# Final norm of a two-layer block: result tile split by token halves, six stores of other sizes, and eight products of ones behind the sums

## The chip, the cores and the metric

The kernel runs on one core of one Trainium2 chip. The metric is the device time of one execution in microseconds. The kernel before takes 2117.86 us (median of 3 runs, 2117.08 to 2118.18). One further execution was profiled; its own time was 2118.3 us, of which 2116.5 us lie between its first and its last instruction (the span).

## The reference

The model has 256 tokens and a width of 2048, all in float32. Layer 0 is a mixer of a 31-tap causal convolution and a multi-scale pooling, then a SwiGLU with 5632 hidden columns. Layer 1 is a gated 3-tap convolution mixer and another SwiGLU. A last RMS norm follows:

```python
def rms_norm(x, g):
    xf = x.astype(jnp.float32)
    y = xf * lax.rsqrt(jnp.mean(xf * xf, axis=-1, keepdims=True) + EPS)
    return (y * g.astype(jnp.float32)).astype(x.dtype)

def reference(...):
    h = x
    for i in range(DEPTH):
        h = h + (conv_pool_mixer(h, ...) if i % 2 == 0 else short_conv_mixer(h, ...))
        h = h + swiglu(rms_norm(h, ffn_norm[i]), w_gate[i], w_up[i], w_down[i])
    return rms_norm(h, final_norm)
```

## The kernel before

**Data.** Activations lie transposed: partition p holds feature 128·c + p of chunk c, and the 256 tokens run along the free axis. `h` is one tile of 128 x 16 chunks x 256 tokens. The output has the same form, so one partition's row in memory is 16 chunks of 256 tokens, 16 KB.

**Weights and main products.** All weights come as 128x128 blocks in the order of use, loaded by SP (`fetch`, L102). Pieces of 8 blocks are split into a rounded part `hi` (ScalarE, L112) and the rest `lo` (VectorE, or GpSimd for part of the first mixer, L119). TensorE multiplies with hi and lo, in three products of 256 columns (L164 to L166) or in two of 512 and 256 columns (L161 and L162). Steps off the main path are put into queues in the code and released as products are issued; the final order on each engine is made by a scheduler that simulates the program, so a small change of one operation can move others.

**Norms.** A norm does not scale its tokens before the products. It collects squares per chunk (`Norm.square`), sums them over the partitions by small products with a tile of ones (`rsqrt_of`, L235: one column per half of the tokens, so token t sits on partition t of column 0 or 1), and computes 1/sqrt there on 2 columns (`spread_over`, L242 to L249): ScalarE takes a square root, VectorE the reciprocal `y`, and one Newton step e = y·(1.5 − 0.5·var·y²). To bring the values back to the free axis, VectorE multiplies the identity by `e` into the tile `diag` (L253, one half of the tokens each) and TensorE multiplies ones with `diag`: one product of 256 columns for the inner norms (`over_features`, L261), two of 128 columns for the last one (L255, `half`), so that each half of the tokens has its own PSUM tile. `spread_over` serves all norms, the layer norm of the first mixer too (`ln_rstd`). A float32 product of this kind is two MATMUL records in the trace.

**The end of the program.** The down projection of the last SwiGLU adds its result to `h` chunk by chunk. The gain of the last norm is multiplied into `h` on the way (L275), so only the factor per token is missing. After the last chunk: add (L311), square (L289), four sum records, the chain of small steps, the two `half` products, and then (L590) VectorE multiplies `h` in place, in ten pieces. Pieces of chunks 0 and 1 come first, one for each half of the tokens, each stored by its own DMA (L594); then chunks 2-3, 4-7, 8-11 and 12-15, two pieces of VectorE for one DMA (L599). `tc.issue_after` holds the order of the pieces. SP issues all six stores.

The program begins with nine products of ones (L214, `WARM`), whose result nobody reads, while the first data is on its way.

Of the kernel before, what the change touches and what calls it, by code (L numbers as in the profile page):

```python
# [3 lines left out]

# [66 lines left out]
AHEAD = 1  # L71

WARM = 9

POOL_SPLIT = range(96, 24 * NC + 16 + 7 * NC + 8)

# [6 lines left out]
def block_kernel(ctx: ExitStack, tc: tile.TileContext, xT: bass.AP, xtok: bass.AP, vec: bass.AP, wall: bass.AP, out: bass.AP):  # L83
    nc = tc.nc
# [4 lines left out]
    tmp = ctx.enter_context(tc.tile_pool(name="tmp", bufs=2))  # L89
    ps = ctx.enter_context(tc.tile_pool(name="ps", bufs=5, space=PSUM))  # L90
# [116 lines left out]
    h = act.tile([P, NC, T], F32, name="h")  # L207
    xs = act.tile([P, NC, 2 * T], F32R, name="xs")
    ones = const.tile([P, P], F32, name="ones")
    nc.gpsimd.memset(ones, 1.0)  # L210

    idle = ps_st.tile([P, P], F32, name="idle", tag="st")
    for _ in range(WARM):
        nc.tensor.matmul(idle, ones, ones, start=True, stop=True)  # L214
# [11 lines left out]
    def rsqrt_of(*totals, scale, halves=False, st=None):  # L226

        small = ps_st.tile([P, 8], F32, name="st", tag="st")  # L230
        if st is None:
            st = small[:, :2]
        for i, x in enumerate(totals):
            for j in range(2):
                nc.tensor.matmul(st[:, j : j + 1], x[:, j * P : (j + 1) * P], ones[:, :1], start=i == j == 0, stop=i == len(totals) - 1, skip_group_check=True)  # L235
        return spread_over(small, st, scale, halves)

    def spread_over(small, st, scale, halves=False):

        var, root, e = (small[:, 2 * i : 2 * i + 2] for i in range(1, 4))  # L240
        y = tmp.tile([P, 2], F32, name="inv", bufs=1)
        nc.scalar.activation(root, st, AF.Sqrt, scale=scale, bias=eps)  # L242
        nc.vector.tensor_scalar(out=var, in0=st, scalar1=scale, scalar2=EPS, op0=ALU.mult, op1=ALU.add)
        nc.vector.reciprocal(y, root)
        for j in range(2):
            yj = y[:, j : j + 1]
            nc.vector.scalar_tensor_tensor(out=e[:, j : j + 1], in0=var[:, j : j + 1], scalar=yj, in1=yj, op0=ALU.mult, op1=ALU.mult)
        nc.vector.tensor_scalar(out=e, in0=e, scalar1=-0.5, scalar2=1.5, op0=ALU.mult, op1=ALU.add)
        nc.vector.tensor_tensor(out=e, in0=e, in1=y, op=ALU.mult)  # L249
        diag = tmp.tile([P, T], F32, name="diag", tag="sq")  # L250
        spread = [ps.tile([P, P], F32, name="half", tag="acc") for _ in range(2)] if halves else None
        for j in range(2):
            nc.vector.tensor_tensor(out=diag[:, j * P : (j + 1) * P], in0=identity, in1=e[:, j : j + 1].broadcast_to([P, P]), op=ALU.mult)  # L253
            if halves:
                nc.tensor.matmul(spread[j], ones, diag[:, j * P : (j + 1) * P], start=True, stop=True)  # L255
        return spread or over_features(diag)

    def over_features(x):

        st = ps_st.tile([P, T], F32, name="st", tag="st")  # L260
        nc.tensor.matmul(st, ones, x, start=True, stop=True)  # L261
        return st

    class Norm:
# [95 lines left out]
    with tc.tile_pool(name="m0", bufs=1) as m0, tc.tile_pool(name="ps_side", bufs=2, space=PSUM) as ps_side:  # L360
# [223 lines left out]
    last = Norm("final_norm", final=True)  # L584
    swiglu(norm, last)
    halves = rsqrt_of(*last.sums, scale=1.0 / D, halves=True)

    def normed(at, n, j):
        part = h[:, at : at + n, j * P : (j + 1) * P]
        return nc.vector.tensor_tensor(out=part, in0=part, in1=halves[j].unsqueeze(1).broadcast_to([P, n, P]), op=ALU.mult).ins  # L590

    for j in range(2):
        start = normed(0, 2, j)
        nc.sync.dma_start(out[:, :2, j * P : (j + 1) * P], h[:, :2, j * P : (j + 1) * P])  # L594
    for at, n in ((2, 2), (4, 4), (8, 4), (12, 4)):
        with tc.issue_after(start):
            for j in range(2):
                start = normed(at, n, j)
        nc.sync.dma_start(out[:, at : at + n, :], h[:, at : at + n, :])  # L599


def _blocks(w):
# [78 lines left out]
```

## Time and profile before

| | before |
|---|---|
| median of 3 runs | 2117.86 us (2117.08 to 2118.18) |
| the profiled execution's own time | 2118.3 us |
| its span | 2116.5 us |
| TensorE (PE) busy | 2091.5 us, 99% |
| VectorE (DVE) busy | 1382.9 us, 65% |
| ScalarE (ACT) busy | 1060.6 us, 50% |
| GpSimd (POOL) busy | 200.7 us, 9% |
| last product of the last projection ends | 2103.0 us after the span's start |
| TensorE clock granted, mean | 0.995 |

Times in the trace count from the span's start. PE is TensorE's products, PEld its weight loads, SPq the issues of DMAs by SP. A row of the timeline gives start, duration, engine, line, operation, tiles and shapes, how many instructions were merged into the row, and in brackets how long the engine had been idle and for whom it waited. A row of a table by stretches gives, for each stretch, its length and each engine's busy time with the number of instructions, then the granted TensorE clock (1.00 is full), the busy share of the DMA engines and GB/s.

### The profile page before, as it was taken

Reading aid. Unit: us, or ns where it says so; the run is one execution under the profiler, and the core shown is the slowest. Engines: PE = TensorE matmul, PEld = TensorE weight load, DVE = VectorE, ACT = ScalarE, POOL = GpSimd, SP = SyncE. Lnnn points to the kernel's source line nnn. Section 1 sums busy time; section 2 is a strip of 40 time slices with the busy share of each in tenths; the row PEclk is TensorE's granted clock in tenths of the full one; section 3 lists DMA queues with packets and bytes.
Section 4 is the critical chain, followed back from the end, with each engine's and each line's share of the span. In section 5 each row is a group of like instructions: output and inputs, shape, how many; then the busy total and the mean of one; then the engine's idle time right before and its main releaser. Section 6 shows DMA issues by size and latency. Waiting matters only on the chain.

```text
span 2116.5 us, 31578 instructions
## 1 busy us (share of the span) xinstructions
PE 2091.5 (99%) x12568; PEld 1860.0 (88%) x12568; DVE 1382.9 (65%) x1983; ACT 1060.6 (50%) x1571; POOL 200.7 (9%) x180
## 2 busy tenths in 40 slices
PE   8999999999999999999999999999999999999997
PEld 8999988888888888888888888888888888888887
DVE  6888766666556666666777777766665556666554
ACT  7776654444444444454444445554444444444453
POOL 3985200000000000011000001100000000000011
PEclk9999999999999999999999999999999999999999
DMA  8554455555555555455455555555555555555551
GB/s 324 190 189 170 149 181 198 181 197 182 196 180 194 184 182 196 180 186 192 179 194 185 197 183 196 180 186 193 190 189 191 187 188 191 179 191 187 181 193 64
DMA packets 57140, 395.53 MB, mean 187 GB/s; under 512 B 6432, under 2 KB 7456, under 8 KB 10016
## 3 DMA queue, kind: packets, MB, share of 16 engines
q1 hardware_dynamic: 56992, 393.52, 52.0%
q8 instruction: 98, 1.61, 0.3%
q14 instruction: 50, 0.41, 0.1%
HBM read 391.39 MB, written 2.10 MB: 186 GB/s over the span
## 4 chain that ended last, share of the span: by engine, by line
PE 98%; DVE 1%; DMA 1%; ACT 0%; SPq 0%; issue 0%; DVEq 0%; ACTq 0%
PE acc L161 57%; PE acc L162 29%; PE acc L164 4%; PE acc L166 4%; PE acc L165 4%; DMA rows<-in_xtok 0%; DMA h<-in_xT 0%; DVE h L590 0%; ACT hi L112 0%; PE st L235 0%; PE st L261 0%; DVE lo L119 0%; SPq L102 0%; ACT conv L468 0%; DVE conv L423 0%
## 5 line engine op out<-in xcount | busy, mean ns | idle before, releaser
L112 ACT CAST hi<-w 128x1024 fp32r<-128x1024 f32 (+1 forms) x740 | 775.1, 1048 | 990.7 <-PE acc L161 628.0
L119 DVE TENSOR_TENSOR lo<-w,hi 128x1024 fp32r<-128x1024 f32 (+1 forms) x691 | 845.2, 1224 | 651.2 <-ACT hi L112 647.1
L161 PE MATMUL acc<-xs,hi 128*128 128x512 f32 x3584 | 1253.9, 395 | 0.0
L162 PE MATMUL acc<-xs,lo 128*128 128x256 f32 x3584 | 1005.4, 281 | 0.0
L161 PEld LDWEIGHTS acc<-xs,hi 128*128 128x128 f32 x3584 | 671.8, 187 | 155.3
L162 PEld LDWEIGHTS acc<-xs,lo 128*128 128x128 f32 x3584 | 677.8, 189 | 0.1
L161 PE MATMUL acc<-y,hi 128*128 128x512 f32 x1386 | 486.7, 395 | 0.0
L162 PE MATMUL acc<-y,lo 128*128 128x256 f32 x1386 | 389.3, 281 | 0.0
L161 PEld LDWEIGHTS acc<-y,hi 128*128 128x128 f32 x1386 | 260.4, 188 | 61.0
L162 PEld LDWEIGHTS acc<-y,lo 128*128 128x128 f32 x1386 | 260.1, 188 | 0.4
L291 POOL TENSOR_TENSOR sumsq<-sumsq,sq 128x256 f32<-128x256 f32 x56 | 59.0, 1054 | 1612.6 <-ACT sq L289 1612.6
L164 PE MATMUL acc<-xs,hi 128*128 128x256 f32 x512 | 144.0, 284 | 5.5 <-ACT hi L112 4.3
L165 PE MATMUL acc<-xs,hi 128*128 128x256 f32 x512 | 143.6, 283 | 0.0
L166 PE MATMUL acc<-xs,lo 128*128 128x256 f32 x512 | 141.2, 284 | 0.1
L119 POOL TENSOR_TENSOR lo<-w,hi 128x1024 fp32r<-128x1024 f32 x49 | 119.1, 2452 | 43.4 <-PE acc L165 34.5
L164 PEld LDWEIGHTS acc<-xs,hi 128*128 128x128 f32 x512 | 98.0, 192 | 6.6 <-ACT hi L112 5.2
L165 PEld LDWEIGHTS acc<-xs,hi 128*128 128x128 f32 x512 | 98.1, 192 | 0.0
L166 PEld LDWEIGHTS acc<-xs,lo 128*128 128x128 f32 x512 | 96.5, 192 | 0.5 <-DVE lo L119 0.5
L161 PE MATMUL acc<-z,hi 128*128 128x512 f32 x256 | 89.4, 394 | 0.0
L186 ACT COPY cross<-acc 128x256 f32<-128x256 f32 x224 | 81.0, 362 | 0.0
L162 PE MATMUL acc<-z,lo 128*128 128x256 f32 x256 | 71.7, 281 | 0.0
L311 DVE TENSOR_TENSOR h<-acc,h 128x256 f32<-128x256 f32 x112 | 47.3, 423 | 19.9 <-PE acc L166 14.1
(131 smaller groups left out, 1201.1 us busy)
## 6 DMA issues: line engine op xcount, KB each, us to landing
w<-in_wall SPq DMA_DIRECT2D x365, 1024.0 KB, 4.8
w<-in_wall SPq DMA_DIRECT2D x7, 512.0 KB, 7.9
rows<-in_xtok SPq DMA_DIRECT2D x2, 1024.0 KB, 7.8
h<-in_xT SPq DMA_DIRECT2D x7, 256.0 KB, 7.3
out<-h SPq DMA_DIRECT2D x3, 512.0 KB, 2.8
v<-in_vec SPq DMA_DIRECT2D x1, 260.0 KB, 6.6
h<-in_xT SPq DMA_DIRECT2D x2, 128.0 KB, 2.4
w<-in_wall SPq DMA_DIRECT2D x1, 256.0 KB, 4.0
```

What stands on the lines that cost most here:

```text
L112: nc.scalar.copy(hi[:, : n * P], w)
L119: engine.tensor_tensor(out=lo[:, : n * P], in0=w, in1=hi[:, : n * P], op=ALU.subtract)
L161: nc.tensor.matmul(acc, hi, x, start=first, stop=False, skip_group_check=True)
L162: nc.tensor.matmul(acc[:, T:], lo, x[:, :T], start=False, stop=last, skip_group_check=True)
L164: nc.tensor.matmul(acc[:, :T], hi, x[:, :T], start=first, stop=False)
L165: nc.tensor.matmul(acc[:, :T], hi, x[:, T:], start=False, stop=False)
L166: nc.tensor.matmul(acc[:, :T], lo, x[:, :T], start=False, stop=last)
L186: nc.scalar.copy(t, acc[:, T:])
L291: nc.gpsimd.tensor_tensor(out=self.sums[0], in0=self.sums[0], in1=sq, op=ALU.add)
L311: nc.vector.tensor_tensor(out=h[:, n, :], in0=acc[:, :T], in1=h[:, n, :], op=ALU.add)
```

## The change

Four things are edited.

1. `rsqrt_of`, only where `halves` is set (the last norm): behind the sum products, TensorE gets `KEEP` = 8 products of ones with ones, 128 columns each, into a PSUM tile of their own that nobody reads. `tc.issue_after` puts them behind the last sum product.
2. `spread_over`, for every norm: the two VectorE instructions of one column each (var·y·y with y as a per-partition scalar) become two instructions of two columns each (y·y into a new tile, then var times that).
3. The end: the result goes to a new tile `res` of 128 x 2 halves x 16 chunks x 128 tokens, not in place. VectorE works through the first half of the tokens in pieces of 2, 6 and 8 chunks, then the second in 8, 6 and 2. Each piece has its own store, with 1, 3, 4, 4, 3 and 1 KB per partition.
4. The output in memory is 128 x 2 x 16 x 128; the host puts the axes back.

```diff
+KEEP = 8
...
         for i, x in enumerate(totals):
             for j in range(2):
-                nc.tensor.matmul(st[:, j : j + 1], x[:, j * P : (j + 1) * P], ones[:, :1], start=i == j == 0, stop=i == len(totals) - 1, skip_group_check=True)
+                mm = nc.tensor.matmul(st[:, j : j + 1], x[:, j * P : (j + 1) * P], ones[:, :1], start=i == j == 0, stop=i == len(totals) - 1, skip_group_check=True)
+        if halves:
+
+            idle = ps.tile([P, P], F32, name="idle", tag="acc")
+            with tc.issue_after(mm.ins):
+                for _ in range(KEEP):
+                    nc.tensor.matmul(idle, ones, ones, start=True, stop=True)
         return spread_over(small, st, scale, halves)
...
-        y = tmp.tile([P, 2], F32, name="inv", bufs=1)
+        y, yy = (tmp.tile([P, 2], F32, name=n, bufs=1) for n in ("inv", "inv2"))
...
-        for j in range(2):
-            yj = y[:, j : j + 1]
-            nc.vector.scalar_tensor_tensor(out=e[:, j : j + 1], in0=var[:, j : j + 1], scalar=yj, in1=yj, op0=ALU.mult, op1=ALU.mult)
+        nc.vector.tensor_tensor(out=yy, in0=y, in1=y, op=ALU.mult)
+        nc.vector.tensor_tensor(out=e, in0=var, in1=yy, op=ALU.mult)
...
-    def normed(at, n, j):
-        part = h[:, at : at + n, j * P : (j + 1) * P]
-        return nc.vector.tensor_tensor(out=part, in0=part, in1=halves[j].unsqueeze(1).broadcast_to([P, n, P]), op=ALU.mult).ins
-
-    for j in range(2):
-        start = normed(0, 2, j)
-        nc.sync.dma_start(out[:, :2, j * P : (j + 1) * P], h[:, :2, j * P : (j + 1) * P])
-    for at, n in ((2, 2), (4, 4), (8, 4), (12, 4)):
-        with tc.issue_after(start):
-            for j in range(2):
-                start = normed(at, n, j)
-        nc.sync.dma_start(out[:, at : at + n, :], h[:, at : at + n, :])
+    with tc.tile_pool(name="fin", bufs=1) as fin:
+
+        res = fin.tile([P, 2, NC, P], F32, name="res")
+        start = None
+        for j, pieces in enumerate((((0, 2), (2, 6), (8, 8)), ((0, 8), (8, 6), (14, 2)))):
+            for at, n in pieces:
+                with tc.issue_after(start) if start is not None else nullcontext():
+                    part = h[:, at : at + n, j * P : (j + 1) * P]
+                    by = halves[j].unsqueeze(1).broadcast_to([P, n, P])
+                    start = nc.vector.tensor_tensor(out=res[:, j, at : at + n, :], in0=part, in1=by, op=ALU.mult).ins
+                nc.sync.dma_start(out[:, j, at : at + n, :], res[:, j, at : at + n, :])
```

Because the scheduler simulates the program, edit 2 also moves a few instructions elsewhere. Line numbers in the changed kernel are 2 to 14 higher than before.

On TensorE, at the first norm of the program (before; `st` is the product that spreads 1/sqrt, `acc` the main products):

```order
L164 MATMUL acc<-xs,hi 128x256
L165 MATMUL acc<-xs,hi 128x256
L166 MATMUL acc<-xs,lo 128x256
L261 MATMUL st<-diag,ones 128x256
L164 MATMUL acc<-xs,hi 128x256
```

On the same engine at the same place, the change has:

```order
L166 MATMUL acc<-xs,hi 128x256
L167 MATMUL acc<-xs,hi 128x256
L268 MATMUL st<-diag,ones 128x256
L168 MATMUL acc<-xs,lo 128x256
L166 MATMUL acc<-xs,hi 128x256
```

The spreading product stands one main product earlier. The same exchange is found at the norms before the two SwiGLUs and the second mixer; at the layer norm the order stays.

On GpSimd, in the first mixer (`sw` and `pm` are steps of the pooling, `lo` pieces of weights; before):

```order
L505 TENSOR_TENSOR sw<-sw 128x2x256
L119 TENSOR_TENSOR lo<-w,hi 128x1024 x2
L507 TENSOR_TENSOR sw<-sw,corr 128x2x15
L119 TENSOR_TENSOR lo<-w,hi 128x1024 x2
L508 TENSOR_TENSOR pm<-sw,pm 128x512
L119 TENSOR_TENSOR lo<-w,hi 128x1024 x3
L505 TENSOR_TENSOR sw<-xp 128x2x262
```

The same place on GpSimd in the change:

```order
L512 TENSOR_TENSOR sw<-sw 128x2x256
L121 TENSOR_TENSOR lo<-w,hi 128x1024 x3
L514 TENSOR_TENSOR sw<-sw,corr 128x2x15
L121 TENSOR_TENSOR lo<-w,hi 128x1024 x2
L515 TENSOR_TENSOR pm<-sw,pm 128x512
L121 TENSOR_TENSOR lo<-w,hi 128x1024 x2
L512 TENSOR_TENSOR sw<-xp 128x2x262
```

One pooling step waits behind one more weight piece; ScalarE and VectorE exchange the neighbours of that pooling group in the same stretch.

On TensorE, the end of the program (before):

```order
L166 MATMUL acc<-y,lo 128x256
L235 MATMUL st<-ones,sumsq 128x1 x2
L235 MATMUL st<-ones,sq 128x1 x2
L255 MATMUL half<-diag,ones 128x128 x2
L676 UNCONDITIONAL_BRANCH
```

The end of TensorE's program in the change:

```order
L168 MATMUL acc<-y,lo 128x256
L237 MATMUL st<-ones,sumsq 128x1 x2
L237 MATMUL st<-ones,sq 128x1 x2
L243 MATMUL idle<-ones 128x128 x8
L262 MATMUL half<-diag,ones 128x128 x2
L681 UNCONDITIONAL_BRANCH
```

The eight products of ones stand ahead of the two `half` products on an engine that works in this order.

More of the change, by code (lines that the diff above doesn't have):

```diff
@@ L1 @@
 from collections import deque
-from contextlib import ExitStack
+from contextlib import ExitStack, nullcontext
 from functools import partial
@@ L674 @@
     args = [nc.dram_tensor(f"in_{n}", a.shape, F32, kind="ExternalInput").ap() for n, a in arrays.items()]
-    args.append(nc.dram_tensor("out_0", (P, NC, T), F32, kind="ExternalOutput").ap())
+    args.append(nc.dram_tensor("out_0", (P, 2, NC, P), F32, kind="ExternalOutput").ap())
     with tile.TileContext(nc, schedule_with_timeline_sim=True) as tc:
@@ L679 @@
     got = np.asarray(r.results[0]["out_0"])
-    return np.ascontiguousarray(got.transpose(2, 1, 0)).reshape(1, T, D)
+    return np.ascontiguousarray(got.transpose(1, 3, 2, 0)).reshape(1, T, D)
```

## The prediction

> **What bounds the kernel now.** I read the page first, then the end of the timeline, then the same stretch by windows with the clock and the DMA share, and last the places where TensorE waits.
>
> From the page:
>
> ```profile
> span 2116.5 us, 31578 instructions
> PE 2091.5 (99%) x12568; PEld 1860.0 (88%) x12568; DVE 1382.9 (65%) x1983; ACT 1060.6 (50%) x1571; POOL 200.7 (9%) x180
> PE 98%; DVE 1%; DMA 1%; ACT 0%; SPq 0%; issue 0%; DVEq 0%; ACTq 0%
> ```
>
> For 99% of the span TensorE's products are the bound, and the change takes none of them away. What can move is the end behind the last main product (2103.0 to 2116.5, 13.5 us) and the few places where a norm makes TensorE wait. All that is 0.6% of the time, so the forecast is a matter of tenths of a microsecond. The timeline of the end:
>
> ```profile
> 2103.94 0.61 PE L235 MATMUL st<-ones,sq 128*128 128x1 f32 x4 [0.63 <-ACT sq L289]
> 2104.58 0.24 ACT L242 ACTIVATE st<-st,eps 128x2 f32<-128x2 f32 x1 [0.16 <-PE st L235]
> 2105.26 0.49 DVE L247 SCALAR_TENSOR_TENSOR st<-st,inv 128x1 f32<-128x1 f32 x2
> 2105.78 0.17 DVE L248 TENSOR_SCALAR st<-st 128x2 f32<-128x2 f32 x1
> 2105.98 0.17 DVE L249 TENSOR_TENSOR st<-st,inv 128x2 f32<-128x2 f32 x1
> 2106.26 0.48 DVE L253 TENSOR_TENSOR diag<-v,st 128x128 f32<-128x128 f32 x2
> 2106.66 0.93 PEld L255 LDWEIGHTS half<-diag,ones 128*128 128x128 f32 x4 [2.20 <-issue]
> 2106.69 1.20 PE L255 MATMUL half<-diag,ones 128*128 128x128 f32 x4 [2.15 <-DVE diag L253]
> 2107.50 5.10 DVE L590 TENSOR_TENSOR h<-h,half 128x256 f32<-128x256 f32 x10 [0.76 <-PE half L255]
> 2107.95 0.92 SPq L594 DMA_DIRECT2D out<-h  x2
> ```
>
> It is one chain: sums, square root, five small steps, diag, half, and then VectorE without a pause for 5.10 us. TensorE stands still for 2.15 us in it. The windows show what that does to its clock (the column behind the busy times; then DMA share and GB/s):
>
> ```profile
> core 0: us, PE busy (x) PEld busy (x) DVE busy (x) ACT busy (x) POOL busy (x), PEclk, DMA share, GB/s
> 2103.22:2106.63 3.41, 0.70 (x5) 0.53 (x5) 1.72 (x9) 1.16 (x3) 0.00 (x0) 1.00 0.00 0
> 2106.63:2110.04 3.41, 1.20 (x4) 0.93 (x4) 2.65 (x7) 0.00 (x0) 0.00 (x0) 0.50 0.29 91
> 2109.00:2110.00 1.00, 0.00 (x0) 0.00 (x0) 1.00 (x3) 0.00 (x0) 0.00 (x0) 0.50 0.87 267
> 2110.70:2111.10 0.40, 0.00 (x0) 0.00 (x0) 0.40 (x2) 0.00 (x0) 0.00 (x0) 0.50 0.15 61
> 2111.10:2112.00 0.90, 0.00 (x0) 0.00 (x0) 0.90 (x3) 0.00 (x0) 0.00 (x0) 0.50 0.97 400
> 2114.00:2115.00 1.00, 0.00 (x0) 0.00 (x0) 0.00 (x0) 0.00 (x0) 0.00 (x0) 0.50 0.91 373
> ```
>
> The clock went from 1.00 to 0.50 at 2106.63, 0.03 us ahead of the weight load of `half`: both `half` products ran at half speed. And the DMA engines, short of work up to 2111.10, are then full to the end. So the last part of the program is bound by 1.57 MB (the last three stores of 512 KB) at about 400 GB/s, counted from the moment when the first of these three is issued. Its issue, the last issue, and SP's wait for the last landing:
>
> ```profile
> 2110.23 0.34 SPq L599 DMA_DIRECT2D out<-h  x1
> 2112.66 0.33 SPq L599 DMA_DIRECT2D out<-h  x1
> SPq L676 <- DMA out<-h: 2.4, 1, 2.4
> out<-h SPq DMA_DIRECT2D x3, 512.0 KB, 2.8
> out<-h SPq DMA_DIRECT2D x2, 128.0 KB, 1.9
> ```
>
> From issue to first bytes lie 0.9 us (2110.23 to 2111.1).
>
> **The small steps (edit 2).** Before, two one-column instructions take from 2105.26 to 2105.78, 0.52 us. Now two two-column ones, each as L248, whose start lies 0.20 us ahead of the next: 0.40. **−0.12 us**. Bounds 0 (if a new tile costs a wait) and −0.15.
>
> The other norms gain this only where TensorE waits for it. At the first norm:
>
> ```profile
> 39.37 0.30 PEld L261 LDWEIGHTS st<-diag,ones 128*128 128x128 f32 x2
> 39.48 0.59 PE L261 MATMUL st<-diag,ones 128*128 128x256 f32 x2
> 41.14 0.36 PE L164 MATMUL acc<-xs,hi 128*128 128x256 f32 x1 [1.07 <-DVE gate L318]
> ```
>
> The spreading product ran right behind the main ones, so `diag` was ready; behind it TensorE stood for 1.07 us until VectorE had freed a PSUM tile. Now it stands one main product earlier, all that hangs on it comes 0.12 us earlier, which is how far apart main products are in the chain of waits there, and the displaced product fills the pause: **−0.12 us**, between 0 and −0.2:
>
> ```profile
> 39.41 0.12 PE acc L165
> ```
>
> At the layer norm (its chain of waits) a weight piece stands between, which hides the gain, **0**:
>
> ```profile
> 206.36 1.05 ACT hi L112
> 207.44 1.23 DVE lo L119
> 208.66 0.41 DVE diag L253 x2
> ```
>
> `lo` waits for `hi`, not for the small steps, and `diag` stands behind `lo`. The other three norms make TensorE wait nowhere: 0.
>
> **The products of ones (edit 1).** Their price is seen at the program's start, at a clock that was low until nearly the last of them:
>
> ```profile
> 0.99 3.70 PE L214 MATMUL idle<-ones 128*128 128x128 f32 x18 [0.99 <-POOL eps L216]
> ```
>
> Eight are 16 records. At low clock 3.70/18 makes 0.206 us each, 3.3 us in all; at full clock L261 (0.59 us for two, the second lasting 0.38) shows 0.21 us between starts at 256 columns, so 0.107 at 128, and 16 take 1.7 us. They start behind the sums at about 2104.5 and are issued by 2106.2; `half` wants to load its weights at 2106.66 − 0.12 = 2106.54. So they lie wholly beside the small steps of ScalarE and VectorE and cost nothing, with 0.3 us to spare; past that each delay goes straight into `half`.
>
> How busy TensorE must be is bounded by the other place where the clock fell, at the layer norm:
>
> ```profile
> 205.40:208.82 3.42, 0.98 (x9) 0.78 (x7) 2.96 (x10) 2.33 (x2) 0.00 (x0) 1.00 0.70 273
> 208.82:219.06 10.24, 6.46 (x26) 5.77 (x27) 5.31 (x10) 6.11 (x12) 0.00 (x0) 0.50 0.29 107
> 215.64:219.06 3.42, 3.42 (x18) 3.42 (x17) 1.90 (x3) 1.62 (x4) 0.00 (x0) 0.50 0.00 0
> ```
>
> A stretch of 3.42 us with TensorE busy for 0.98 of it, 29%, was followed by a low clock. In that of 2103.22 to 2106.63 TensorE was busy for 0.70 us, 20%; now it would be 0.70 + 1.7 = 2.4 of 3.41 us, 70%. I take it that the clock stays. Then `half`: before, from the weight load (2106.66) to VectorE's start (2107.50) 0.84 us, all but 0.04 of it TensorE. At full clock, halving gives 0.40; L261's 0.71 us (39.37 to 40.07) less 2 x 0.107 for the halved columns gives 0.50. I take 0.45: **−0.35 us** (−0.30 to −0.40; 0 if the clock falls anyway).
>
> The Trainium skill (TensorE: Matmul & The Clock Gate, "What's actually happening") has the gate watch a free-running window of 3413 ns that does not reset at the kernel's start. The trace agrees in the length, since the low stretch in the middle is 10.24 us, three such windows. By the page the step would fall elsewhere in other executions; what that does is the first rival.
>
> **The pieces (edit 3).** VectorE's rows for pieces of 512 columns, and one instruction of 1024 with another output tile than its input:
>
> ```profile
> 2109.52 3.07 DVE L590 TENSOR_TENSOR h<-h,half 128x512 f32<-128x512 f32 x5
> L119 DVE TENSOR_TENSOR lo<-w,hi 128x1024 fp32r<-128x1024 f32 (+1 forms) x691 | 845.2, 1224 | 651.2 <-ACT hi L112 647.1
> ```
>
> Five starts of 512 columns are (3.07 − 0.68)/4 = 0.60 us apart; 256 columns, from the seven starts ahead, 0.33. That is 0.07 + 1.04 ns per column: 0.87 for 768, 1.13 for 1024 columns. The sum over all is 4.7 us and not 5.1, but VectorE's end no longer decides. What counts is when the store is issued from which the DMA engines stay full. Before, 2110.20 − 2107.50 = 2.70 us behind VectorE's start. Now the third store, behind pieces of 256, 768 and 1024: 0.33 + 0.87 + 1.22 = 2.41. **−0.29 us** (with the first two stores, 0.5 MB, out just by then: the second is issued 1.3 us behind the start, and takes 0.9 + 1.0 us, until 3.2; the third's first bytes come at 3.3).
>
> From there the same 1.57 MB are left (512 + 512 + 384 + 128 KB). Each later store is issued before the one ahead is through, so the engines stay full; SP issues six stores as before, at 0.33 to 0.46 us each, and the two closest come 0.33 us apart, ahead of a full queue. Only the last 128 KB go in rows of 1 KB: the rows of 512 bytes went at 267 GB/s (2109 to 2110), rows of 4 KB at 400; between the two, 0.40 us for 0.33: **+0.05 us** (0 to +0.15).
>
> Sum: −0.12 − 0.12 − 0.35 − 0.29 + 0.05 = **−0.83 us**. Against its own execution that is a span of 2115.7 us and a time of 2117.5; against the median of the runs, which lies 0.44 us below the profiled one, 2117.86 − 0.83 = **2117.0 us**.
>
> **Rivals.**
>
> *The clock was not what the profile shows.* The step came 0.03 us ahead of `half`; a shift of the window by 0.8 us to a later time leaves `half` fast without any help, and then edit 1 brings nothing: −0.83 + 0.35 = −0.48, 2117.4 us. The same time comes out if a window that is 70% busy still loses the clock. For it: no row here shows a window between 29% and full that kept it. Against it: the profiled execution is one like the others.
>
> *The last store decides, not the throughput.* Then the end is the last issue plus its landing: VectorE's start at 2107.50 − 0.12 − 0.35 = 2107.03, 4.75 us of pieces, issue at 2111.8, and 1.9 us for 128 KB give 2113.7, against 2112.66 + 2.8 = 2115.5 before: −1.8, with the first norm −1.9, 2116.0 us. Against it: the DMA share of 0.91 to 0.97 in the last windows, which says that a store of 128 KB would queue.
> The Trainium skill (DMA: Bandwidth & Descriptors, "Rules for kernel authors") speaks against stores this small: at least 1 MiB per DMA, small ones joined. Here 512 KB in one store went at 400 GB/s, so the rows agree only for the smallest pieces. By that page's fit for one DMA (2.0 us plus the bytes at 436 GB/s, given for GpSimd's path) 128 KB would take an estimated 2.3 us and the kernel 2116.4 us in this case.
>
> *Slower: the products of ones hold `half` back.* Place: TensorE, which works in order, from 2104.5 on. If the clock falls before they are through, or they start late, `half` waits. At low clock 16 x 0.206 = 3.3 us end at 2107.8, `half` starts 1.15 us later than before and is slow: +1.15 − 0.29 + 0.05 − 0.12 = +0.8, 2118.7 us. The kernel is slower than before from the point where `half` starts 0.36 us late, that is from 0.16 us per record on. Against it: the clock was 1.00 until 2106.63, and the eight products themselves fill the window.
>
> *Slower: the moved order in the first mixer makes TensorE wait.* GpSimd now does three pieces of `lo` in a row ahead of a pooling step:
>
> ```profile
> 70.03 4.82 POOL L119 TENSOR_TENSOR lo<-w,hi 128x1024 fp32r<-128x1024 f32 x2
> PE acc L164 <- DVE xs L198: 0.9, 1, 0.9
> ```
>
> One piece more is 2.4 us, −0.83 + 2.4 = +1.6, 2119.4 us if all of it reaches TensorE. Against it: the one wait of that mixer between the first norm and the layer norm is these 0.9 us, and it is for VectorE.
>
> **How the numbers follow.** The forecast gets 0.62, the clock 0.17, the last store 0.10, the late `half` 0.06, the moved order 0.05. Runs scatter: a stretch of low clock as in the middle of the program (208.82 to 219.06) may be one window of 3.41 us longer or shorter by where it begins, and with products 3.42/18 = 0.19 us apart and not 0.12 that is some 1.3 us; the three runs span 1.1 us. So the range is 2115.8 (the last store, less 0.2) to 2118.4 (the forecast with its costs at their worst, +0.5, and half that scatter). About 0.2%, 4.2 us, is what a measurement of this kernel can tell from no change, and no case reaches it: within it 0.96, faster 0.02, slower 0.02.
>
> **What would show it.** `idle` is through before `half` loads its weights, and the clock is 1.00 while `half` runs: from `diag`'s start to VectorE's about 0.9 us (1.24 before). VectorE starts near 2107.0 counted from a last main product at 2103.0. DMA share is near 1 from the third store to the end, and the last landing is some 0.7 us nearer to the last product. The forecast is wrong if DMA runs dry between the stores, if `half` waits for `idle`, or if TensorE has a new wait before 206.

## The result, and the profile after

The changed kernel takes 2104.66 us (median of 4 runs: 2103.73, 2104.31, 2105.01, 2109.83), the kernel before in the same series 2117.72 us (4 runs, 2117.08 to 2118.18). The ratio is 0.9944 (95% interval 0.9926 to 0.9961): 13 us faster, not 0.83. The profiled execution took 2103.73 us.

Span, busy times and one group of main products, from the page of the changed kernel (the columns of the group: busy time and mean ns of one, then idle time before them):

```profile
span 2102.0 us, 31608 instructions
PE 2079.1 (99%) x12584; PEld 1855.8 (88%) x12584; DVE 1383.4 (66%) x1979; ACT 1060.9 (50%) x1571; POOL 200.6 (10%) x180
L163 PE MATMUL acc<-xs,hi 128*128 128x512 f32 x3584 | 1243.3, 391 | 0.0
```

The same group in the kernel before:

```profile
L161 PE MATMUL acc<-xs,hi 128*128 128x512 f32 x3584 | 1253.9, 395 | 0.0
```

Of the 14.5 us between the two spans, 12.4 are in TensorE's busy time, although TensorE has 16 records more. The same 3584 products cost 10.6 us less. So the main products themselves became faster, and nothing in the prediction allows for that.

**Where the time went.** With the starts of the main products of both traces laid side by side, one by one, the changed kernel gains at four places: 2.9 us at the layer norm of the first mixer and behind it (209 to 286 us), 5.8 us in the second token half of the first SwiGLU and its down projection (628 to 995), 5.6 us at the same place of the second SwiGLU (1721 to 2089), and 0.6 us behind the last product. It loses 0.3 us in the down projection of each first token half. Elsewhere it moves by less than 0.5 us. Three stretches of 100 us, by windows for TensorE alone, show the second place and the third. The first row lies in a first token half, the others lie in the second halves of the two SwiGLUs. The columns are the stretch, its length, PE busy with the number of products, granted clock, DMA share and GB/s. Before:

```profile
300.00:400.00 100.00, 100.00 (x579) 1.00 0.54 190
740.00:840.00 100.00, 100.00 (x568) 1.00 0.52 185
1850.00:1950.00 100.00, 100.00 (x568) 1.00 0.52 185
```

After:

```profile
300.00:400.00 100.00, 100.00 (x579) 1.00 0.53 190
740.00:840.00 100.00, 100.00 (x579) 1.00 0.54 190
1850.00:1950.00 100.00, 100.00 (x578) 1.00 0.54 190
```

TensorE is busy for 100% at a clock of 1.00 in all six rows, and yet the kernel before gets 568 products done in its second halves where it does 579 in its first half. Instructions, shapes and order on TensorE are the same in both kernels there. From the starts in the trace, a pair of products (512 and 256 columns) takes 346.7 ns at the fast pace and 353.3 ns at the slow one. The slow pace is a pattern of its own: starts lie 233, 117, 241, 120, 236 and 113 ns apart, again and again, where the fast one has 230 and 117. A second half has 704 pairs, so 6.6 ns make 4.65 us, and its projection adds up to 1.2 us (352 pairs at 353.3 against 350.0).

**The layer norm.** The rows of the windows (busy times of PE, PEld, DVE, ACT and POOL, then clock, DMA share, GB/s) of the changed kernel:

```profile
205.91:209.32 3.41, 0.59 (x5) 0.35 (x3) 2.46 (x7) 2.33 (x2) 0.00 (x0) 1.00 0.59 240
209.32:216.15 6.83, 3.44 (x15) 2.90 (x14) 3.60 (x6) 5.53 (x12) 0.00 (x0) 0.50 0.43 155
```

The low clock lasts 6.83 us here, 10.24 us before: one window of 3.41 us less. In all executions profiled without products of ones at this place it was 6.83 or 10.24 us, both lengths under the code of before with an edit or none, so this part belongs to the execution and not to the change. But it is only some 1.4 of the 2.9 us. Behind it come the products of the first mixer's output projection that read the tile `cat`, and their pace changed too. By windows at full clock, before:

```profile
222.00:257.00 35.00, 35.00 (x294) 1.00 0.50 179
```

After:

```profile
222.00:257.00 35.00, 35.00 (x302) 1.00 0.50 181
```

From the starts in the traces, two of these products (256 columns each) take 240.0 ns before and 233.3 ns after, which is 1.2 us over the 352 products that run behind the low clock in both. The last 0.3 us lie at the start of the first token half.

**The end.** One row of the timeline of before that the prediction did not show, the last add:

```profile
2103.01 0.42 DVE L311 TENSOR_TENSOR h<-acc,h 128x256 f32<-128x256 f32 x1 [6.41 <-PE acc L166]
```

The timeline of the changed kernel's end:

```profile
2088.73 0.28 PE L168 MATMUL acc<-y,lo 128*128 128x256 f32 x1
2089.05 0.42 DVE L318 TENSOR_TENSOR h<-acc,h 128x256 f32<-128x256 f32 x1 [6.55 <-PE acc L168]
2089.97 0.61 PE L237 MATMUL st<-ones,sq 128*128 128x1 f32 x4 [0.62 <-ACT sq L296]
2090.44 2.03 PE L243 MATMUL idle<-ones 128*128 128x128 f32 x16
2091.30 0.16 DVE L253 TENSOR_TENSOR inv<-inv 128x2 f32<-128x2 f32 x1
2091.49 0.17 DVE L254 TENSOR_TENSOR st<-st,inv 128x2 f32<-128x2 f32 x1
2091.69 0.17 DVE L255 TENSOR_SCALAR st<-st 128x2 f32<-128x2 f32 x1
2092.17 0.48 DVE L260 TENSOR_TENSOR diag<-v,st 128x128 f32<-128x128 f32 x2
2092.57 0.52 PEld L262 LDWEIGHTS half<-diag,ones 128*128 128x128 f32 x4 [0.29 <-PE idle L243]
2092.60 0.68 PE L262 MATMUL half<-diag,ones 128*128 128x128 f32 x4
2093.10 4.75 DVE L603 TENSOR_TENSOR res<-h,half 128x256 f32<-128x256 f32 x6 [0.45 <-PE half L262]
```

The issue of the third store, in the same timeline for SP alone:

```profile
2095.54 0.33 SPq L604 DMA_DIRECT2D out<-res  x1
```

From the add to VectorE's first piece: 4.05 us, 4.49 before. `half` from weight load to VectorE: 0.53, 0.84 before. The third store is issued 2.44 us behind VectorE's start. The windows of the end:

```profile
2086.66:2090.07 3.41, 2.79 (x25) 2.70 (x23) 0.42 (x1) 0.53 (x2) 0.00 (x0) 1.00 0.00 0
2090.07:2093.48 3.41, 3.08 (x24) 2.73 (x24) 1.87 (x10) 0.63 (x2) 0.00 (x0) 1.00 0.00 0
2093.48:2096.89 3.41, 0.00 (x0) 0.00 (x0) 3.41 (x5) 0.00 (x0) 0.00 (x0) 1.00 0.56 215
2096.70:2097.60 0.90, 0.00 (x0) 0.00 (x0) 0.90 (x2) 0.00 (x0) 0.00 (x0) 0.61 1.04 414
2099.90:2100.20 0.30, 0.00 (x0) 0.00 (x0) 0.00 (x0) 0.00 (x0) 0.00 (x0) 0.50 0.87 297
2100.20:2100.50 0.30, 0.00 (x0) 0.00 (x0) 0.00 (x0) 0.00 (x0) 0.00 (x0) 0.50 0.65 222
```

The clock is 1.00 through `half` and falls only at 2096.89, when nothing on TensorE is left. The two falls of this trace, at 209.32 and 2096.89 us, lie 1887.57 us apart, which is 553 stretches of 3.413 us, so the first three rows are cut at the places where the clock could step. `half` and VectorE's start lie ahead of 2093.48, and the window that ended at 2090.07 was filled by main products. In this execution `half` would thus have had the full clock without the products of ones as well. The DMA engines are full from the third store's first bytes (2096.4) to 2099.9. In the last 0.6 us, when the rows of 1 KB of the last store go out, the rate is 297 and then 222 GB/s.

### The profile page after: what moved, and what is told of

Its sections match the earlier page's. It is cut to its first block, busy times and chain, and to the rows that moved or that the text cites. A ratio compares the mean times of both kernels' runs of the same rounds, so it can differ in the third digit from the quotient of the medians.

```text
span 2102.0 us, 31608 instructions
## 1 busy us (share of the span) xinstructions
PE 2079.1 (99%) x12584; PEld 1855.8 (88%) x12584; DVE 1383.4 (66%) x1979; ACT 1060.9 (50%) x1571; POOL 200.6 (10%) x180
## 4 chain that ended last, share of the span: by engine, by line
PE 98%; DMA 1%; DVE 1%; ACT 0%; SPq 0%; issue 0%; DVEq 0%; ACTq 0%
PE acc L163 57%; PE acc L164 30%; PE acc L166 4%; PE acc L168 4%; PE acc L167 4%; DMA rows<-in_xtok 0%; DMA h<-in_xT 0%; DVE res L603 0%; ACT hi L114 0%; PE st L237 0%; PE st L268 0%; DVE lo L121 0%; SPq L104 0%; ACT conv L475 0%; PE idle L243 0%
```

## The experiments

**What moved.** The new tile of edit 2 has 8 bytes per partition and takes a slot of 32 in its pool. In the built program all that is allocated behind it lies 32 bytes higher (addresses are read from the program; the traces have none). `y` and `z`, the inputs of the down projections and of the second mixer's output projection, go from 159104 (a multiple of 64) to 159136. `cat`, an input of the first mixer's output projection, goes from 184640 to 184672, and other steps of the mixers move as well. The SwiGLU's input `xs` and the weight pieces stay where they were.

The gain could come from the four edits themselves or from the moved tiles. For the moved tiles there were two readings, called A1 and A2 below. In A1 the products fall into one of two rhythms, by the phase at which something breaks their stream, and the address only chose that phase. In A2 the address itself sets the pace.

### The shift alone

Kernel before, with the reciprocal's tile 10 columns wide and not 2; nothing else:

```diff
-        y = tmp.tile([P, 2], F32, name="inv", bufs=1)
+        y = tmp.tile([P, 10], F32, name="inv", bufs=1)[:, :2]
```

> The kernel before with one edit: the tile `inv` is 10 columns wide and not 2, of which 2 are used. Every instruction and its order on TensorE, VectorE and ScalarE stay; all tiles behind `inv` in the scratch memory, y and z among them, lie 32 bytes further on, as in the changed kernel. Theory A (the place of the tiles in memory sets TensorE's pace in the projections from y and z and in the loops that follow them): second halves of both SwiGLUs at 0.347 us a pair and not 0.354, about 2105.3 us (the changed kernel's 2104.7 and the 0.6 us of its end). Theory B (the moved order of instructions, or the new small steps, made the gain): 2117.7 us, as before. Theory C (the pace is a matter of luck in each execution): single runs spread between 2105 and 2118.

Measured 2106.32 us (2104.13 to 2107.52); before on the same chip 2118.1 (median of 19 runs); ratio 0.9942 (0.9927 to 0.9957). Second halves ran at 346.7 ns, and the products that read `cat` at 235.5 ns for two. In the trace every engine has the same instructions in the same order as before. Eight unused columns give nearly the whole gain.

### The four edits without the shift

The changed kernel, with the new tile in the slot of the reciprocal, so that `y` and `z` lie as before:

```diff
-        y, yy = (tmp.tile([P, 2], F32, name=n, bufs=1) for n in ("inv", "inv2"))
+        both = tmp.tile([P, 4], F32, name="inv", bufs=1)
+        y, yy = both[:, :2], both[:, 2:]
```

> The changed kernel with one edit: the new tile `inv2` lies in the free bytes behind `inv`, so that y and z lie where they lay before; all four edits of the change stay, with the order that they bring. Theory A: second halves at 0.354 us a pair again, 2117.1 us (before, less 0.55 at the end and 0.12 to 0.2 at the first norm). Theory B: 2104.7 us. Theory C: spread.

Measured 2116.88 us (10 runs, 2116.14 to 2121.05), ratio 0.9997 (0.9987 to 1.0007). Its second half, by windows:

```profile
740.00:840.00 100.00, 100.00 (x568) 1.00 0.53 189
```

The slow pace is back, and the products that read `cat` are at 240.0 ns for two again. The median lies 1.2 us below that of the kernel before in the same series, and 0.1 us from the forecast of 2117.0. The interval, from 2.8 us faster to 1.5 us slower, contains the predicted 0.83 but does not tell it from zero. The order of the instructions on all four engines is the changed kernel's here, so it costs or brings no more than that.

### Which tile, and by how much

Kernel before, with only `y` and `z` (and what lies behind them) moved up by 32 bytes. The second and third kernel move them by 64 and by 16:

```diff
-            y = fp.tile([P, NH, 2 * T], F32R, name="y")
+            y = fp.tile([P, NH * 2 * T + 8], F32R, name="y")[:, 8:].rearrange("p (n t) -> p n t", n=NH)
...
-        z = m1.tile([P, NC, 2 * T], F32R, name="z")
+        z = m1.tile([P, NC * 2 * T + 8], F32R, name="z")[:, 8:].rearrange("p (n t) -> p n t", n=NC)
```

> The kernel before with y and z (and the `cross` tiles behind them) 32 bytes further on, by 8 unused columns at their start; the tiles of the scratch pool ahead of them stay where they were. If it is the place of y and z, which TensorE reads: 2105.3 us. If it is the place of the scratch tiles (gate, val, sq, diag), which VectorE and ScalarE write: 2117.7 us.

> The kernel before with y and z (and `cross`) 64 bytes further on and not 32. If what counts is whether they start on a multiple of 64 bytes: slow as before, 0.353 us a pair in the second halves, 2118 us. If any other place than the one before does it: 0.347 us a pair, 2106 us.

> The kernel before with y and z 16 bytes further on. If the step that counts is 32 bytes: slow as before, 2118 us, with the projections at 0.349 us a pair. If any place off the multiple of 64 bytes does it: projections at 0.350, second halves at 0.347 us a pair, 2106 us.

| `y`, `z` moved by | time, us | ratio to before (95%) | projection of the first half, ns per pair | second halves, ns per pair |
|---|---|---|---|---|
| 0 (before) | 2118.1; 2117.8 in the series of 16 and 64 bytes | 1 | 348.9 | 353.3 |
| 16 bytes | 2106.92 (2 runs) | 0.9949 (0.9929 to 0.9968) | 350.0 | 346.7 |
| 32 bytes | 2106.45 (4 runs) | 0.9944 (0.9930 to 0.9959) | 350.0 | 346.7 |
| 64 bytes | 2118.39 (8 runs) | 1.0004 (0.9993 to 1.0014) | 351.1 | 353.3 |

For the second halves it is the place of `y` and `z`. The products that read `cat`, which did not move, stayed at 240.0 ns for two in all three. But the second halves do not read `y`. They only write it, and they follow the projection that reads it. That projection got slower where they got faster. This speaks for A1, that the projection hands its rhythm on, but does not show it.

### Breaking the stream

If the second halves have only slipped into a rhythm, something that breaks the stream should change it, with every address as before. In two more kernels, a product of ones that nobody reads was put ahead of each second half of the kernel before, of 128 columns in one and of 256 in the other. The edit of the second:

```diff
+                if half:
+                    idle = ps_st.tile([P, T], F32, name="idle", tag="st")
+                    nc.tensor.matmul(idle, ones, v[:, :T], start=True, stop=True)
```

> The kernel before with one product of ones (two records, 0.2 us) ahead of the second half of each SwiGLU, between the last product that reads y and the first that reads xs; every address stays. If the slow pace of the second halves is a pattern that the loop takes over from the projection ahead of it and keeps as long as nothing breaks the stream of products: those loops at 0.347 us a pair, 5 us less for each SwiGLU (704 pairs by 0.007), some 10 us in all with a share of the projections behind them, 2107 to 2109 us. If the pace comes from the addresses alone, with no memory of what went ahead: 2117.9 us.

> The kernel before with one float32 product of 256 columns (the form of the norms' spreading product) ahead of the second half of each SwiGLU; every address stays. In all traces so far the stream is at 0.347 us a pair behind such a product, whereas behind the product of 128 columns of e4 it came back at 0.353. Theory A1 (the pace is a pattern that the stream of products enters by what goes ahead of it and then keeps): second halves at 0.347 us a pair, 2 x 704 pairs by 0.0066 us = 9.3 us less, and the projections behind them at 0.349 as behind the first halves, 2 x 352 x 0.0043 = 3.0 us less; together 2106 us. Theory A2 (the pace of each loop follows from addresses alone, so from y being written at another place while the loop runs): 2118 us.

2118.17 us, ratio 1.0003 (0.9993 to 1.0012), and 2119.06 us, ratio 1.0008 (0.9998 to 1.0017). Second halves at 353.3 in both: the simple form of A1, that any break at the entry frees the stream, fell.

Then the product of 256 columns was put inside the second half, behind its 18th pair, and in two more kernels one and two pairs later:

```diff
+            def kick(k):
+                if k == 1:
+                    idle = ps_st.tile([P, T], F32, name="idle", tag="st")
+                    nc.tensor.matmul(idle, ones, v[:, :T], start=True, stop=True)
...
-                    (acc_u,) = matmul_chunks(xs, every, wide=True)
+                    (acc_u,) = matmul_chunks(xs, every, wide=True, behind=kick if half and f == 0 else None)
```

> The kernel before with one float32 product of 256 columns in the second half of each SwiGLU, 18 pairs into its first loop (in e5 it stood ahead of the first pair). In the loops that are fast, the norm's spreading product of this form stands in mid-loop behind a slow stretch with the same three-pair rhythm (0.241 + 0.120 as the last pair), and the fast rhythm begins behind it; 18 pairs in, the last pair has that form here. Theory A1 (a rhythm that the stream falls into and keeps): 0.347 us a pair from there to the end of the loop, 0.349 in the projection behind it, 2106 us. Theory A2 (addresses alone): 0.353, 2118 us.

> As e9, one pair later, so that the last pair ahead has the second form of the rhythm. Theory A1 does not say which of the three places falls into the fast rhythm, only that not all three need to agree; theory A2: 0.353 us a pair, 2118 us.

> As e9, two pairs later: the third form of the rhythm. Theory A1: as e10; theory A2: 0.353 us a pair, 2118 us.

One run each: 2106.74, 2118.71 and 2118.82 us; before on the same chip 2118.42 (median of 7). Two stretches of the second halves by windows, behind the 18th pair:

```profile
740.00:840.00 100.00, 100.00 (x579) 1.00 0.54 190
1850.00:1950.00 100.00, 100.00 (x579) 1.00 0.54 190
```

One pair later:

```profile
740.00:840.00 100.00, 100.00 (x568) 1.00 0.53 185
1850.00:1950.00 100.00, 100.00 (x568) 1.00 0.52 183
```

The timeline of TensorE around the added product, in the kernel that has it behind the 18th pair:

```profile
636.72 0.40 PE L161 MATMUL acc<-xs,hi 128*128 128x512 f32 x1
636.96 0.28 PE L162 MATMUL acc<-xs,lo 128*128 128x256 f32 x1
637.08 0.59 PE L540 MATMUL idle<-v,ones 128*128 128x256 f32 x2
637.32 0.58 PE L161 MATMUL acc<-xs,hi 128*128 128x512 f32 x1
637.74 0.28 PE L162 MATMUL acc<-xs,lo 128*128 128x256 f32 x1
637.85 0.40 PE L161 MATMUL acc<-xs,hi 128*128 128x512 f32 x1
```

One product that costs 0.4 us of TensorE's time (it and the next pair take 0.77 us, from 637.08 to 637.85, a pair alone 0.35), with every address as before, takes 11.7 us off the kernel; the same product one pair later takes off nothing. In the trace each of the three kernels has both its second halves at one pace from the added product on. So A2, the address by itself, fell for the second halves, and A1 holds in this form: where the break stands decides. The slow rhythm repeats every three pairs and three neighbouring places were tried, so that it is the phase in this cycle is inferred. A fourth place, three pairs behind the first, was not tried.

The trace of before shows such a turn by itself. Its first SwiGLU half begins with pairs of 350, 361 and 349 ns, again and again (mean 353), and runs at 346.7 from behind the spreading product of the norm (281.88 us) on, with the same tiles throughout.

### The products of ones, and the low clock at the layer norm

The changed kernel with `KEEP` = 0:

> The changed kernel without the eight products of ones (KEEP = 0). Theory (they keep the clock up for `half`): from the first weight load of `half` to VectorE's start 0.84 us as before if the low clock has come by then, and not 0.53; about 2105 us in all, since 0.3 us is less than the runs scatter. Rival (the clock would not have fallen by then): 0.5 us in this profile too.

2105.51 us (2 runs, 2105.38 and 2105.63), ratio to before 0.9942 (0.9922 to 0.9962). The timeline of its end:

```profile
2094.14 0.93 PEld L262 LDWEIGHTS half<-diag,ones 128*128 128x128 f32 x4 [2.08 <-issue]
2094.97 1.28 DVE L603 TENSOR_TENSOR res<-h,half 128x256 f32<-128x256 f32 x2 [0.75 <-PE half L262]
```

It is 0.83 us from weight load to VectorE here and 0.53 in the changed kernel, but these two profiles differ in where the clock could step: here at 2092.88, ahead of `half`, there at 2093.48, behind it. The clock does not always fall in time: in three kernels without the products (the shift alone, `y` and `z` by 32 bytes, the product behind the 18th pair) it was still 1.00 at `half`, which then took 0.53 us as well. A profile in which the products did count is that of the four edits without the shift. There a window ended just ahead of `half` (2105.57 us):

```profile
2101.47:2104.88 3.41, 2.78 (x26) 2.70 (x25) 1.26 (x6) 1.16 (x3) 0.00 (x0) 1.00 0.00 0
```

The products of ones in its timeline:

```profile
2103.44 2.03 PE L243 MATMUL idle<-ones 128*128 128x128 f32 x16
```

The clock stayed at 1.00 and `half` took 0.53 us. Without the products 1.34 of the 2.78 us are left, by an estimate from the two rows, and in all traces every window at full clock with less than 1.5 us of work was followed by the low clock. So they bring 0.3 us in some executions, and none in others.

The same means at the layer norm, added to the changed kernel: 11 and 13 products of ones in the two pauses.

```diff
+        idle = ps.tile([P, P], F32, name="idle", tag="acc")
+        for after, n in zip((last_product[0], spreading[-1]), KEEP_LN):
+            with tc.issue_after(after.ins):
+                for _ in range(n):
+                    nc.tensor.matmul(idle, ones, ones, start=True, stop=True)
```

> The changed kernel with 24 more products of ones in the two pauses of TensorE at the layer norm (11 ahead of the spreading product, 13 behind it), so that TensorE is busy there. If the low clock behind these pauses (6.8 to 10.2 us long in the profiles) costs what the traces say, 2.2 to 3.1 us, it goes away: no stretch of 0.50 before the end, 2102 us. If the products run into the chain behind them they delay it by up to 1 us: 2103 to 2105 us. If the low clock costs nothing there: 2104.7 us.

Its windows at the layer norm:

```profile
205.91:209.32 3.41, 3.41 (x32) 3.41 (x31) 2.58 (x9) 1.55 (x3) 0.00 (x0) 1.00 0.72 228
209.32:216.15 6.83, 5.97 (x48) 5.49 (x47) 4.63 (x8) 4.90 (x9) 0.00 (x0) 1.00 0.52 193
```

The clock stays at 1.00, and from the product with which that mixer's output projection begins (158.18 us in the changed kernel, 160.10 here) to the first down projection 345.3 us pass, not 346.7. But the time is 2104.6 us (4 runs, 2102.41 to 2105.21; ratio to before 0.9929, 0.9913 to 0.9946), not to be told from the changed kernel. In the profiled execution the clock fell twice for 3.41 us at the start, at 8.7 and at 25.8 us, which cost some 2 us there.

### All together at the old addresses

The four edits with the new tile in the reciprocal's slot, the product behind the 18th pair of the second halves, and the products of ones at the layer norm; beside it the changed kernel once more, on the same chip:

> The changed kernel with all four edits, but with every moved tile back at its address of before (the new tile shares the slot of the reciprocal), plus the one product of ones behind the 18th pair of each second half and the products of ones in the two pauses at the layer norm. Theory (the pace is set by the phase at which something breaks the stream, and the address only chose that phase): second halves 346.7 ns per pair, the projections behind them 348.9 and not 350.0, so some 4 x 352 + 256 pairs x 1.1 ns = 1.8 us less than the changed kernel, no low clock at the layer norm: 2102.5 to 2103. Rival (the address does the work, the product of ones only happened to hit it in the kernel before): second halves at 353.3 and 2115 to 2117, as with the same edits at the old address without the product.

> The changed kernel once more, beside the last one on the same chip. Theory: 2104.0 to 2105.5, with the second halves at 346.7 ns per pair. If the pace is chosen anew in each execution and not by the program, some runs lie 4 to 6 us higher (one second half of 704 pairs x 6.6 ns = 4.6 us, and its projection), as the one execution of 2109.8 did.

2104.85 us (5 runs: 2103.8, 2104.38, 2104.85, 2106.38, 2109.61), ratio 0.9941 (0.9929 to 0.9954). The changed kernel: 2104.47 us (5 runs, 2103.33 to 2108.17), ratio 0.9938 (0.9925 to 0.9952). So with another way into the fast rhythm the old addresses reach the changed kernel's time. They do not pass it by the 1.5 us expected. The projections did run at 348.9 ns and gained 0.3 to 0.4 us each, but in each second half, where the added product stands, 0.5 us went back. And the products that read `cat`, at its old place, ran at 240.0 ns for two: at full clock in both, the 384 of them took 46.3 us, against 45.1 in the changed kernel with the products of ones at the layer norm. These 1.2 us the expectation had left out.

The profiled execution was the one of 2109.61 us, and it shows what such an outlier is. Windows for TensorE in the first half and in the second half:

```profile
300.00:400.00 100.00, 100.00 (x568) 1.00 0.52 189
740.00:840.00 100.00, 100.00 (x579) 1.00 0.54 190
```

Here it is the first half of the first SwiGLU, fast in every other kernel, that runs at 353.3 ns up to its projection. Laid beside the changed kernel that costs 4.5 us, and 2109.61 less 4.5 is 2105.1, among the four other runs (2103.80 to 2106.38). It looks as if the same program runs at either pace, so that the rhythm is not fixed by the code. None of the four faster runs was profiled, so this is inferred from their times. The 2109.83 and 2108.17 us of the changed kernel fit one half at the slow pace (4.65 us and part of a projection), but neither was profiled.

## Why the prediction was wrong

**The step that failed** is the first: "For 99% of the span TensorE's products are the bound, and the change takes none of them away. What can move is the end behind the last main product (2103.0 to 2116.5, 13.5 us) and the few places where a norm makes TensorE wait." The number of products did not change; their pace did. The 2 x 704 pairs of the second halves and the projections behind them make 11.4 of the 14.5 us between the profiles, and the products that read `cat` 1.2, against 0.6 lost in the projections of the first halves. The sum has no term for this. The trace of before had a hint: the stretches by windows give 568 products in 100 us in the second halves and 579 in the first, at the same clock and with the same 100% busy. The prediction read the busy share, which cannot show it, and named edit 2 only by its instructions, not by the tile that it adds ahead of others.

The size of that term could not have been forecast: which of the two rhythms a shift would choose was not to be read from the trace of before. But the case "a second half changes its pace" could have been a rival at 4.65 us per half, and the range of 2115.8 to 2118.4, which ends 11 us above the result, would have had to reach to it.

**The terms that were there**, in the profiles:

| term | predicted, us | measured, us |
|---|---|---|
| small steps of the last norm | −0.12 | −0.12 (0.20 per instruction) |
| first norm | −0.12 | −0.13 |
| `half` at full clock | −0.35 | −0.31 (0.84 to 0.53; the 0.50 of the row L261 was nearer than the halving), in this execution by where the clock stepped |
| third store after VectorE's start | −0.29 (2.41, from 2.70) | −0.29 (2.44, from 2.73: the row of the issue has 2110.23, not 2110.20) |
| last bytes | +0.05 | +0.13 (third store's issue to the last landing 5.35, 5.22 before) |
| sum | −0.83 | −0.72 |

The first norm is as forecast: its spreading product stands ahead of one more main product, and the wait behind it is shorter.

```profile
39.28 0.59 PE L268 MATMUL st<-diag,ones 128*128 128x256 f32 x2
39.52 0.47 PE L168 MATMUL acc<-xs,lo 128*128 128x256 f32 x1
40.94 0.36 PE L166 MATMUL acc<-xs,hi 128*128 128x256 f32 x1 [0.95 <-DVE gate L325]
```

The last bytes cost more than the forecast and stayed inside its bounds (0 to +0.15). In the trace of the DMA engines the 128 KB of the last store move within the last 0.6 us of the transfers, where the prediction had put 0.40 us. The 16 records of products of ones took 2.03 us and not 1.7, which cost nothing, since they were through before `half`.

**What would show it.** `idle` ended 0.1 us ahead of `half`'s weight load (0.3 expected), the clock was 1.00 at `half`, `diag` to VectorE took 0.93 us (0.9 expected), and the last landing came 0.6 us nearer to the last product (0.7 expected). All of these held, and all concerned the end. Nothing in that list looked at the pace of the main products.

**The rivals.** *The clock was not what the profile shows*: a case that does occur, in three of the kernels without products of ones, and by the place of the steps in the changed kernel's profile too. Its condition, that the window lies so that `half` is fast without help, held there, so the −0.31 us are in part luck of that execution. Its price is too small to be seen in the times. The prediction also held, for this rival, that no row showed a window between 29% and full that kept the clock; the trace of before has one of 48% (1.64 of 3.41 us, 21.09 to 24.50). *The last store decides*: no; the last store landed 2.9 us behind its issue and not 1.9, so it queued behind the ones ahead. *The products of ones hold `half` back*: no, they were through before. *The moved order makes TensorE wait*: no; the main products up to 209 us differ by 0.2 us, and the four edits at the old addresses took 2116.88 us.

**Scatter.** The low clock at the layer norm was put at 1.3 us per window. Between the two profiles one window less went with 2.9 us, of which some 1.4 remain for the window once the pace of the products that read `cat` (1.2) and the start of the first half (0.3) are taken off: the size was about right.

## What to carry to other kernels

Busy share and clock do not show the pace of a saturated engine: count its instructions in equal stretches of one kernel, and where like loops differ, suspect a rhythm before the work. A new tile of 8 bytes moves every address behind it; build a change also with its old addresses before its gain is credited to its code. And a pace that one extra product can turn can be lost again by the next edit, so measure it as a term of its own each time.

## What the runs showed of the hardware

- A stream of weight loads and products of 512 and 256 columns, with all operands ready and the clock at 1.00, had two stable paces, 346.7 and 353.3 ns per pair (1.9% apart). It stayed in one for hundreds of pairs, and one added product, at one of three neighbouring places, turned it from the slow one to the fast one (2106.74 us against 2118.71 and 2118.82). A first half that is fast in the other 15 profiles was slow in one. The Trainium skill (TensorE: Matmul & The Clock Gate, "Back-to-back issue gap") gives N/2.4 + 2.5 ns for a product by itself, an estimated 325 ns for such a pair, and says that weight loads and products together set the spacing in a stream; the trace shows more than that sum, and two values. Why there are two, and what in the machine holds the slow one, stays open.
- The pace of the first halves' projections went with where their moving operand lies: 348.9 ns per pair at 159104, a multiple of 64 bytes, 350.0 at 16 or 32 bytes beyond, 351.1 one step of 64 further. The address alone does not fix it: behind a slow second half the same projection at 159104 ran at 353.3. The products that read `cat`, of 256 columns, took 240.0 ns for two with `cat` at 184640 and 233.3 or 235.5 at 184672. Whether the address or a rhythm does this was not tried. Why two places that are both multiples of 64 (348.9 and 351.1) differ stays open too.
- Within each trace the steps of the clock lay on one grid of 3.413 us (1887.57 us, 553 stretches, between the two falls of the changed kernel). The clock fell behind windows of this grid in which TensorE was busy for 0.59 of 3.41 us (17%, 205.91 to 209.32 of the changed kernel) and even 2.05 us (60%, 2089.47 to 2092.88 with `KEEP` = 0). It stayed behind windows of 1.64 us (48%, 21.09 to 24.50 before) and 1.73 us (51%, 21.59 to 25.00 of the changed kernel). In all these traces, windows at full clock with less than 1.5 us lost it, windows with more than 2.1 us kept it, and between the two the busy time alone does not decide. The Trainium skill (the same page, "What's actually happening") names an idle window as the condition; by these rows it need not be idle. All low stretches ahead of the end were 3.41, 6.83 or 10.24 us long, and where they began differed from execution to execution.
